# Opening of a one-core decoder layer: weights laid out by channel tile, conditioning rows earlier in the load queue, dummy products first, two evictions behind roundings

## The chip, the core and the metric

The kernel runs on one core of a Trainium2 chip. The core has a matrix engine (PE, with its weight loads shown as PEld), a vector engine (DVE), a scalar engine (ACT), a general engine (POOL) and a queue that issues most transfers (SP). Sixteen DMA engines move data between the chip's memory (HBM) and the core's buffers. PE writes into eight accumulation banks (PSUM), which DVE and ACT read.

The metric is the device time of one execution in microseconds (us), taken as the median of several runs.

## The reference

One layer of a conditioned decoder at batch 1, 256 positions, width 2048, in 32-bit floats:

```
mod = silu(c) @ w_ada + b_ada                 # six vectors of 2048: shift1, scale1, gate1, shift2, ...
h   = rmsnorm(x, g1) * (1 + scale1) + shift1
proj = h @ w_in                               # 2048 -> 10752: lru_x, lru_gate, q, k, v, gate_a, gate_b
y_a = (rg_lru(conv4(lru_x)) * gelu(lru_gate)) @ w_lru_out
y_b = window_attention(q, k, v) @ w_attn_out
x  += gate1 * ((sigmoid(g_a) * y_a + sigmoid(g_b) * y_b) @ w_out)
h2  = rmsnorm(x, g2) * (1 + scale2) + shift2
x  += gate2 * (relu(h2 @ w_ff1) ** 2 @ w_ff2)
out = rmsnorm(x, final_g)
```

What matters here is the first part: the conditioning vectors `mod`, the normed input `h`, and the first products of `w_in`.

## The kernel before, in words

**Tiles.** Channels lie on the 128 partitions, so a width of 2048 is 16 channel tiles (k = 0 to 15) and the 10752 outputs of `w_in` are 84 output tiles (f). An activation tile is 128 x 256. Most products are made with rounded operands: a weight tile is split into a rounded part `wh` (ACT, line 174) and a remainder `wl` (DVE, line 179), an activation into `h[:, 0]` and `h[:, 1]`, and three products replace one (lines 200 to 202). A few products take the plain 32-bit weights as they come from memory; each is then two PE instructions, and needs no rounding.

**Order.** Instructions of the opening are pinned: each engine takes them as they are written in the program. SP issues loads in program order, and a load waits until the buffer that it fills is free. Loads of 1 MB (`raw` tiles: conditioning rows `ra` and weights `rw`) share four buffers.

**The opening** computes all that the first products need:

- SP loads the identity, conditioning row 0 (`ra`, 1 MB), the input x in four pieces of 512 KB (`wh` and `wl` buffers), and row 1. ACT issues two small loads of vectors.
- PE lays silu(c) out along the partitions (16 transposes, line 247), and then runs dummy products of a tile of ones (`WARM`, line 281) that nobody reads.
- DVE multiplies each conditioning row with silu(c) and sums it (`ada_unit`, line 267). Two rows give shift and scale of one channel tile k; `norm1_gain` (line 323) makes the factor.
- x is scaled (lines 295, 297), transposed on PE in four quarters (`turn_in`, line 307) and taken out of PSUM by ACT (`take_in`, line 313).
- For channel tile k, ACT applies factor and shift and rounds (`norm1_tile`, lines 328 and 330); DVE makes the remainder (`norm1_rest`, line 334).
- The "front": ten output tiles (units 0 and 1 of five each) are multiplied with plain weights, one channel tile after the other, as soon as that tile is normed: `front_gemm(0)`, `(1)`, `(2)` (line 361), ten products each into five PSUM banks `fps`. Four of these banks belong to the pool `pg`, which the later products use too.
- `first_part` (line 444) takes the front's sums out of PSUM on ACT, and `split_unit` (lines 174, 179) rounds the weights of unit 2, from which on the products are the rounded ones (`gemm`, lines 200 to 202).

**Passes.** `PASSES` says how the first 56 output tiles are cut: a first pass over channel tiles 0 to 2 (units of five output tiles, a unit being one `raw` load of 128 x 1920), a second pass over channel tiles 3 to 7 (units of three). Between units DVE works off further conditioning rows (`ADA_STEPS`). The remaining channel tiles follow with the rest of the layer, which is not touched.

**Front weights before.** They lie in HBM in the form of units: a partition's row holds, for each output tile, three blocks of 128 floats, one for each channel tile. `front_dma` (lines 351 and 354) picks the blocks of one channel tile out of such rows, in pieces of 512 bytes (the load of 128 x 256 in pieces of 1 KB). It is called for channel tile 0, then, after two conditioning rows, for tiles 1 and 2 together.

Of the kernel before, what the change touches and what calls it, by code (L numbers as in the profile page):

```python
# [10 lines left out]
F32 = mybir.dt.float32  # L11
# [6 lines left out]
P = 128  # L18
T = 256
KT = 16  # L20
# [11 lines left out]
SSD = 4  # L32
WARM = 24

# [7 lines left out]

PASSES = [(0, 3, 56), (3, 8, 56)]
FRONT = 2
PLAIN = {18, 24}
# [17 lines left out]
def hybrid_layer(ctx: ExitStack, tc: tile.TileContext, x, xt, wada, w_p, w_r, w_f, vec, lruw, relb,  # L63
                 onehot, maskc, ident, out):
    nc = tc.nc
# [13 lines left out]
    def nm(s):  # L79
        cnt[0] += 1  # L80
        return f"{s}{cnt[0]}"

    def pair(dt=F32):
        return kp.tile([P, 2, T], dt, tag="k2", name=nm("k"))
# [18 lines left out]
    def ada_dma(pin=same):  # L103
        raw = wp.tile([P, KT * P], F32, tag="raw", name=nm("ra"), bufs=RAW_BUFS)
        pin(nc.sync.dma_start(out=raw, in_=wada[ada_next[0] + len(ada_raw)]))
        ada_raw.append(raw)
# [153 lines left out]
    def ada_unit(pin=same):  # L260
# [8 lines left out]
        return n  # L269

    for q in range(4):
        pc = line_quarter(q)
        o = scr[:, q * 512:(q + 1) * 512]
        if q < 2:
            pin(ve.tensor_copy(o, pc))
        else:
            pin(se.activation(o, pc, AF.Copy))

    wps = pg.tile([P, 2, P], F32, tag="pg", name=nm("pg"))
    for _ in range(WARM):  # L280
        pin(te.matmul(wps[:, 0], lhsT=ones, rhs=ones, start=True, stop=True))
    ada_unit(pin)
# [31 lines left out]

    def warm(n):
        for _ in range(n):
            pin(te.matmul(wps[:, 0], lhsT=ones, rhs=ones, start=True, stop=True))

    h = [None] * KT
# [12 lines left out]
    def norm1_rest(j):  # L332
# [4 lines left out]
    p_units = [(k0, k1, u, min(KT // (k1 - k0), n - u))  # L337
               for k0, k1, n in PASSES for u in range(0, n, KT // (k1 - k0))]
    K1 = PASSES[0][1]
    NF = KT // K1  # L340
    front = {}

    def front_dma(ks):

        t = {k: [pair().rearrange("p a (b m) -> p (a b) m", m=P) for _ in range(FRONT)] for k in ks}
        r = pair().rearrange("p a (b m) -> p (a b) m", m=P)
        n = len(ks)
        src = w_p[0:FRONT, :, 0:NF * K1 * P].rearrange("u p (f k m) -> p u f k m", k=K1, m=P)
        for u in range(FRONT):
            for k in ks:  # L350
                pin(nc.sync.dma_start(out=t[k][u], in_=src[:, u, 0:4, k]))
                for f in range(4):
                    front[u * NF + f, k] = t[k][u][:, f]
            pin(nc.sync.dma_start(out=r[:, u * n:(u + 1) * n], in_=src[:, u, 4, ks[0]:ks[0] + n]))
            for i, k in enumerate(ks):
                front[u * NF + 4, k] = r[:, u * n + i]

# [5 lines left out]

    front_dma([0])
    ada_dma(pin)
    ada_dma(pin)
    front_dma([1, 2])
    scale_in(0, 0)
    scale_in(1, 0)
    turn_in(0)  # L370
    take_in()
    warm(4)
    ada_unit(pin)
# [6 lines left out]
    turn_in(1)  # L380
    ada_dma(pin)
    ada_unit(pin)
    norm1_rest(0)
    ada_unit(pin)
    ada_dma(pin)
    norm1_gain(1)
# [73 lines left out]
    def ask(room):  # L460
        while asked[0] < min(taken[0] + room, len(jobs)):
            i = jobs[asked[0]]
            asked[0] += 1
            if i is None:
                ada_dma(pin)
            else:
                k0, k1, u, nf = p_units[i]
                n = nf * (k1 - k0) * P
                raws[i] = w_dma(w_p[i, :, 0:n], n, pin)

# [52 lines left out]
    split_w = {FRONT: split_unit(FRONT)}  # L523
    take_in()
    for f in range(0, FRONT * NF, 2):
        first_part(fps[f // 2], f)
    open_ps = [None]
    for i in range(FRONT, len(p_units)):
        k0, k1, u, nf = p_units[i]
        if i + 1 < len(p_units):  # L530
            split_w[i + 1] = split_unit(i + 1)
        w = split_w.pop(i)
        for j in range(nf):
# [620 lines left out]
```

## Time and profile before

| what | value |
|---|---|
| median of 3 runs | 1582.1 us (1581.04 to 1583.88) |
| the profiled execution, its own time | 1580.79 us |
| its span (first to last instruction) | 1579.0 us |
| PE busy | 1551.8 us, 98% |
| DVE busy | 1200.7 us, 76% |
| ACT busy | 880.0 us, 56% |
| read from HBM | 384.13 MB, 245 GB/s over the span |

All times below count from the span's first instruction. The profiled execution is 1.8 us longer than its span, and 1.3 us shorter than the median. PE is busy from about the 45th microsecond almost to the end; the share of the first 40th of the span (39.5 us) is 7 tenths, that of all others but the last 9 or more. A row of the timeline or of the chain of waits begins with the start in us and the duration in us. A plain 32-bit product stands there as two PE records, so ten products are 20 records.

### The profile page before, as it was taken

Reading aid. Unit: us, or ns where it says so; the run is one execution under the profiler, and the core shown is the slowest. Engines: PE = TensorE matmul, PEld = TensorE weight load, DVE = VectorE, ACT = ScalarE, POOL = GpSimd, SP = SyncE. Lnnn points to the kernel's source line nnn. Section 1 sums busy time; section 2 is a strip of 40 time slices with the busy share of each in tenths; the row PEclk is TensorE's granted clock in tenths of the full one; section 3 lists DMA queues with packets and bytes.
Section 4 is the critical chain, followed back from the end, with each engine's and each line's share of the span. In section 5 each row is a group of like instructions: output and inputs, shape, how many; then the busy total and the mean of one; then the engine's idle time right before and its main releaser. Section 6 shows DMA issues by size and latency. Waiting matters only on the chain.

```text
span 1579.0 us, 24900 instructions
## 1 busy us (share of the span) xinstructions
PE 1551.8 (98%) x9904; PEld 1393.6 (88%) x9904; DVE 1200.7 (76%) x1841; ACT 880.0 (56%) x1466; POOL 0.2 (0%) x4
## 2 busy tenths in 40 slices
PE   7999999999999999999999999999999999999998
PEld 6999988899988888888889988888888888888887
DVE  5798888899999788798898877865565556655665
ACT  4653457777886564444466763356434663356554
POOL 0000000000000000000000000000000000000000
PEclk9999999999999999999999999999999999999999
DMA  9899976467677768777877666955555555555551
GB/s 362 320 377 344 348 259 222 166 226 254 260 260 277 286 244 298 293 271 290 322 288 260 238 241 242 346 213 188 189 189 190 188 187 190 190 189 188 187 189 57
DMA packets 63717, 387.89 MB, mean 246 GB/s; under 512 B 6800, under 2 KB 14960, under 8 KB 21616
## 3 DMA queue, kind: packets, MB, share of 16 engines
q1 hardware_dynamic: 58896, 381.65, 66.0%
q10 hardware_dynamic: 4704, 4.65, 1.0%
q8 instruction: 77, 1.26, 0.3%
q14 instruction: 40, 0.33, 0.1%
HBM read 384.13 MB, written 2.15 MB: 245 GB/s over the span
## 4 chain that ended last, share of the span: by engine, by line
PE 92%; DVE 4%; DMA 2%; SPq 1%; ACT 1%; issue 0%; DVEq 0%; ACTq 0%
PE pg L214 45%; PE pg L213 22%; PE pg L200 6%; PE pg L202 6%; PE pg L201 5%; PE pg L216 1%; DVE wl L179 1%; PE pg L884 1%; PE pg L885 1%; PE pg L886 1%; DVE ra L267 1%; DVE t L655 1%; PE pg L541 1%; DVE t L682 1%; DMA k<-in_w_p_dram 1%
## 5 line engine op out<-in xcount | busy, mean ns | idle before, releaser
L214 PE MATMUL pg<-k,wh 128*128 128x512 f32 x3088 | 1068.0, 395 | 0.3 <-DVE k L163 0.3
L179 DVE TENSOR_TENSOR wl<-rw,wh 128x1024 fp32r<-128x1024 f32 (+2 forms) x517 | 623.3, 1213 | 276.3 <-ACT wh L174 270.3
L213 PE MATMUL pg<-k,wl 128*128 128x256 f32 x2895 | 810.4, 280 | 0.0
L174 ACT ACTIVATE wh<-rw 128x1024 fp32r<-128x1024 f32 (+2 forms) x517 | 538.7, 1048 | 476.1 <-PE pg L214 327.3
L214 PEld LDWEIGHTS pg<-k,wh 128*128 128x128 f32 x3088 | 566.8, 188 | 119.2 <-PE pg L214 0.6
L213 PEld LDWEIGHTS pg<-k,wl 128*128 128x128 f32 x2895 | 545.1, 188 | 9.7 <-ACT k L162 0.7
L200 PE MATMUL pg<-k,wh 128*128 128x256 f32 x836 | 237.6, 285 | 2.4 <-ACT k L444 1.2
L202 PE MATMUL pg<-k,wl 128*128 128x256 f32 x836 | 235.1, 283 | 2.0 <-DVE wl L179 2.0
L267 DVE CUSTOM_DVE_ANT_0 ra<-ra,scr,vc 128x2048 f32<-128x2048 f32 x96 | 225.2, 2345 | 15.6 <-DMA ra<-in_wada_dram 13.8
L201 PE MATMUL pg<-k,wh 128*128 128x256 f32 x836 | 236.3, 283 | 0.0
L200 PEld LDWEIGHTS pg<-k,wh 128*128 128x128 f32 x836 | 158.3, 189 | 3.9 <-ACT wh L174 1.5
L202 PEld LDWEIGHTS pg<-k,wl 128*128 128x128 f32 x836 | 157.8, 189 | 4.0 <-DVE wl L179 2.2
L201 PEld LDWEIGHTS pg<-k,wh 128*128 128x128 f32 x836 | 158.3, 189 | 0.5 <-issue 0.3
L999 DVE SCALAR_TENSOR_TENSOR k<-pg,mod,k 128x256 f32<-128x256 f32 x124 | 59.9, 483 | 27.8 <-PE pg L214 25.8
L901 ACT ACTIVATE t<-t 128x256 f32<-128x256 f32 x55 | 23.0, 418 | 71.9 <-DVE t L221 71.8
L221 DVE TENSOR_TENSOR t<-pg,t 128x256 f32<-128x256 f32 x131 | 54.7, 417 | 0.3 <-ACT t L220 0.3
L216 PE MATMUL pg<-k,wl 128*128 128x256 f32 x193 | 54.1, 280 | 0.0
L220 ACT ACTIVATE t<-pg 128x256 f32<-128x256 f32 x131 | 47.8, 365 | 0.3 <-PE pg L214 0.3
L216 PEld LDWEIGHTS pg<-k,wl 128*128 128x128 f32 x193 | 36.2, 188 | 8.4
L885 PE MATMUL pg<-z,wh 128*128 128x256 f32 x144 | 40.9, 285 | 0.0
L884 PE MATMUL pg<-z,wh 128*128 128x258 f32 x144 | 40.8, 284 | 0.0
L886 PE MATMUL pg<-z,wl 128*128 128x258 f32 x144 | 40.6, 283 | 0.0
(185 smaller groups left out, 970.5 us busy)
## 6 DMA issues: line engine op xcount, KB each, us to landing
rw<-in_w_f_dram SPq DMA_DIRECT2D x204, 1024.0 KB, 4.8
ra<-in_wada_dram SPq DMA_DIRECT2D x96, 1024.0 KB, 6.3
rw<-in_w_r_dram SPq DMA_DIRECT2D x28, 1024.0 KB, 5.1
rw<-in_w_p_dram SPq DMA_DIRECT2D x27, 960.0 KB, 6.6
bt<-ud ACTq DMA_DIRECT2D x8, 512.0 KB, 4.3
lw<-in_lruw_dram SPq DMA_DIRECT2D x4, 512.0 KB, 5.7
k<-in_x_dram SPq DMA_DIRECT2D x8, 256.0 KB, 5.6
out_dram<-t SPq DMA_DIRECT2D x7, 256.0 KB, 2.6
```

What stands on the lines that cost most here:

```text
L174: pin(se.activation(wh[:, :c], raw[:, o:o + c], AF.Copy))
L179: pin(ve.tensor_tensor(out=wl[:, :c], in0=raw[:, o:o + c], in1=wh[:, :c].bitcast(F32), op=ALU.subtract))
L200: te.matmul(ps, lhsT=wh[:, w], rhs=hl[:, 0], start=k == 0, stop=False)
L201: te.matmul(ps, lhsT=wh[:, w], rhs=hl[:, 1], start=False, stop=False)
L202: te.matmul(ps, lhsT=wl[:, w], rhs=hl[:, 0], start=False, stop=k == n - 1)
L213: te.matmul(ps[:, 0], lhsT=wl[:, w], rhs=hl[:, 0], start=False, stop=False)
L214: te.matmul(ps, lhsT=wh[:, w], rhs=hl, start=k == 0, stop=k == n - 1)
L216: te.matmul(ps[:, 0], lhsT=wl[:, w], rhs=hl[:, 0], start=False, stop=False)
L267: pin(ve.tensor_tensor_reduce(out=raw, in0=raw, in1=scr, scale=1.0, scalar=vc[:, V_BADA + c:V_BADA + c + 1], op0=ALU.mult, op1=ALU.add, ac ...
L884: te.matmul(ps, lhsT=wh[:, e], rhs=z[k][:, 0:258], start=k == 0, stop=False)
L885: te.matmul(ps[:, 0:256], lhsT=wh[:, e], rhs=z[k][:, 258:514], start=False, stop=False)
L999: ve.scalar_tensor_tensor(out=x1[f], in0=ps[:, i], scalar=mod[:, 5 * KT + f:5 * KT + f + 1], in1=x1[f], op0=ALU.mult, op1=ALU.add)
```

## The change

Five edits, all in the opening:

1. **Layout.** The plain weights of the front lie in HBM by channel tile: three rows of `w_p` are added in front, one for each of channel tiles 0, 1, 2, holding ten blocks of 128 floats side by side. `front_dma` loads a channel tile in three pieces (4, 4 and 2 output tiles) of 2 KB, 2 KB and 1 KB for each partition.
2. **Queue order.** The rows for channel tile 2 (`ra_257` and `ra_262` before, `ra_207` and `ra_263` now) stand ahead of the front's weights of tile 2 in SP's queue.
3. **Dummy products.** Six are run ahead of the 16 transposes of silu(c); `WARM` goes from 24 to 26, and the later group of four becomes six.
4. **Evictions.** `take_in` for the last quarter of x moves from ahead of the front's evictions to behind the rounding of unit 3.
5. `PASSES`, `p_units` and the index of `w_p` are adapted to the added rows; later units are loaded as before.

```diff
-WARM = 24
+EARLY, WARM = 6, 26
...
-PASSES = [(0, 3, 56), (3, 8, 56)]
-FRONT = 2
+FRONT, K1 = 2, 3
+NF = KT // K1
+PASSES = [(k, k + 1, FRONT * NF) for k in range(K1)] + [(0, K1, 56), (K1, 8, 56)]
...
+    wps = pg.tile([P, 2, P], F32, tag="pg", name=nm("pg"))
+
+    def warm(n):
+        for _ in range(n):
+            pin(te.matmul(wps[:, 0], lhsT=ones, rhs=ones, start=True, stop=True))
+
+    warm(EARLY)
     for q in range(4):
         pc = line_quarter(q)
...
-    wps = pg.tile([P, 2, P], F32, tag="pg", name=nm("pg"))
-    for _ in range(WARM):
-        pin(te.matmul(wps[:, 0], lhsT=ones, rhs=ones, start=True, stop=True))
+    warm(WARM)
...
-    def front_dma(ks):
-
-        t = {k: [pair().rearrange("p a (b m) -> p (a b) m", m=P) for _ in range(FRONT)] for k in ks}
-        r = pair().rearrange("p a (b m) -> p (a b) m", m=P)
-        n = len(ks)
-        src = w_p[0:FRONT, :, 0:NF * K1 * P].rearrange("u p (f k m) -> p u f k m", k=K1, m=P)
-        for u in range(FRONT):
-            for k in ks:
-                pin(nc.sync.dma_start(out=t[k][u], in_=src[:, u, 0:4, k]))
-                for f in range(4):
-                    front[u * NF + f, k] = t[k][u][:, f]
-            pin(nc.sync.dma_start(out=r[:, u * n:(u + 1) * n], in_=src[:, u, 4, ks[0]:ks[0] + n]))
-            for i, k in enumerate(ks):
-                front[u * NF + 4, k] = r[:, u * n + i]
+    def front_dma(k):
+        n = FRONT * NF
+        t = [pair().rearrange("p a (b m) -> p (a b) m", m=P) for _ in range(0, n, 4)]
+        for f in range(0, n, 4):
+            m = min(4, n - f)
+            pin(nc.sync.dma_start(out=t[f // 4][:, 0:m], in_=w_p[k, :, f * P:(f + m) * P].rearrange("p (f m) -> p f m", m=P)))
+            for i in range(m):
+                front[f + i, k] = t[f // 4][:, i]
...
-    front_dma([0])
+    front_dma(0)
     ada_dma(pin)
     ada_dma(pin)
-    front_dma([1, 2])
+    front_dma(1)
+    ada_dma(pin)
     scale_in(0, 0)
     scale_in(1, 0)
     turn_in(0)
     take_in()
-    warm(4)
+    warm(6)
...
     turn_in(1)
     ada_dma(pin)
+    front_dma(2)
     ada_unit(pin)
     norm1_rest(0)
     ada_unit(pin)
-    ada_dma(pin)
...
     turn_in(3)
     split_w = {FRONT: split_unit(FRONT)}
-    take_in()
     for f in range(0, FRONT * NF, 2):
         first_part(fps[f // 2], f)
...
         if i + 1 < len(p_units):
             split_w[i + 1] = split_unit(i + 1)
+        take_in()
         w = split_w.pop(i)
```

**What it moves in SP's queue.** SP before, from conditioning row 2 to the weights of unit 3 (`ra` are conditioning rows, `k` the front's weights, `rw` the weights of units 2 and 3):

```order
L105 DMA ra_190<-in_wada_dram 128x2048
L105 DMA ra_192<-in_wada_dram 128x2048
L351 DMA k_194<-in_w_p_dram 128x4x128
L351 DMA k_196<-in_w_p_dram 128x4x128
L354 DMA k_198<-in_w_p_dram 128x256
L351 DMA k_195<-in_w_p_dram 128x4x128
L351 DMA k_197<-in_w_p_dram 128x4x128
L354 DMA k_198<-in_w_p_dram 128x256
L105 DMA ra_257<-in_wada_dram 128x2048
L105 DMA ra_262<-in_wada_dram 128x2048
L169 DMA rw_300<-in_w_p_dram 128x1920
L169 DMA rw_302<-in_w_p_dram 128x1920
```

The same place now:

```order
L106 DMA ra_197<-in_wada_dram 128x2048
L106 DMA ra_199<-in_wada_dram 128x2048
L348 DMA k_201<-in_w_p_dram 128x512
L348 DMA k_202<-in_w_p_dram 128x512
L348 DMA k_203<-in_w_p_dram 128x256
L106 DMA ra_207<-in_wada_dram 128x2048
L106 DMA ra_263<-in_wada_dram 128x2048
L348 DMA k_265<-in_w_p_dram 128x512
L348 DMA k_266<-in_w_p_dram 128x512
L348 DMA k_267<-in_w_p_dram 128x256
L170 DMA rw_310<-in_w_p_dram 128x1920
L170 DMA rw_312<-in_w_p_dram 128x1920
```

Rows 4 and 5 (`ra_207`, `ra_263`) went from behind the weights of both tiles to between those of tile 1 and those of tile 2; a channel tile's weights are three loads of whole rows, where six gathered loads held two tiles.

**What it moves on ACT.** ACT before, from the rounding of unit 2 on (L174 rounds weights, L313 takes the transposed x out of PSUM, L444 the front's sums):

```order
L174 ACTIVATE wh_339<-rw_300 128x1024
L174 ACTIVATE wh_341<-rw_300 128x896
L313 ACTIVATE k_348<-pa_325 128x512
L313 ACTIVATE k_350<-pa_330 128x512
L444 ACTIVATE k_352<-pg_230 128x512
L444 ACTIVATE k_354<-pg_231 128x512
L444 ACTIVATE k_356<-pg_232 128x512
L444 ACTIVATE k_358<-pg_233 128x512
L444 ACTIVATE k_360<-pa_234 128x512
L174 ACTIVATE wh_364<-rw_302 128x1024
L174 ACTIVATE wh_366<-rw_302 128x896
```

And now (the same operations are L175, L319 and L439):

```order
L175 ACTIVATE wh_349<-rw_310 128x1024
L175 ACTIVATE wh_351<-rw_310 128x896
L439 ACTIVATE k_358<-pg_236 128x512
L439 ACTIVATE k_360<-pg_237 128x512
L439 ACTIVATE k_362<-pg_238 128x512
L439 ACTIVATE k_364<-pg_239 128x512
L439 ACTIVATE k_366<-pa_240 128x512
L175 ACTIVATE wh_370<-rw_312 128x1024
L175 ACTIVATE wh_372<-rw_312 128x896
L319 ACTIVATE k_378<-pa_335 128x512
L319 ACTIVATE k_380<-pa_340 128x512
```

The two evictions of the last quarter of x stood ahead of the front's five and now stand behind unit 3's rounding. DVE's order is the same as before, and PE's differs by the dummy products and by which buffers the front's products read.

More of the change, by code (lines that the diff above doesn't have):

```diff
@@ L313, in take_in @@
             pin(se.activation(xs[-1].rearrange("p a b -> p (a b)"), turned_in.pop(0), AF.Copy))
-    def warm(n):
-        for _ in range(n):
-            pin(te.matmul(wps[:, 0], lhsT=ones, rhs=ones, start=True, stop=True))
     h = [None] * KT
@@ L337, in hybrid_layer @@
     p_units = [(k0, k1, u, min(KT // (k1 - k0), n - u))
-               for k0, k1, n in PASSES for u in range(0, n, KT // (k1 - k0))]
-    K1 = PASSES[0][1]
-    NF = KT // K1
+               for k0, k1, n in PASSES[K1:] for u in range(0, n, KT // (k1 - k0))]
     front = {}
-    def front_dma(ks):
-        t = {k: [pair().rearrange("p a (b m) -> p (a b) m", m=P) for _ in range(FRONT)] for k in ks}
-        r = pair().rearrange("p a (b m) -> p (a b) m", m=P)
-        n = len(ks)
-        src = w_p[0:FRONT, :, 0:NF * K1 * P].rearrange("u p (f k m) -> p u f k m", k=K1, m=P)
-        for u in range(FRONT):
-            for k in ks:
-                pin(nc.sync.dma_start(out=t[k][u], in_=src[:, u, 0:4, k]))
-                for f in range(4):
-                    front[u * NF + f, k] = t[k][u][:, f]
-            pin(nc.sync.dma_start(out=r[:, u * n:(u + 1) * n], in_=src[:, u, 4, ks[0]:ks[0] + n]))
-            for i, k in enumerate(ks):
-                front[u * NF + 4, k] = r[:, u * n + i]
+    def front_dma(k):
[6 more added lines that the diff above has]
+                front[f + i, k] = t[f // 4][:, i]
     def front_gemm(k):
@@ L468, in ask @@
                 n = nf * (k1 - k0) * P
-                raws[i] = w_dma(w_p[i, :, 0:n], n, pin)
+                raws[i] = w_dma(w_p[K1 + i, :, 0:n], n, pin)
     def take():
```

## The prediction

> **What bounds the kernel now.** I first cut the span into stages. A row holds the stretch in us, its length, then busy us (and records) of PE, PEld, DVE, ACT and POOL, the granted PE clock, the DMA engines' share and GB/s.
>
> ```profile
> 0.00:44.00 44.00, 31.31 (x164) 28.15 (x164) 23.97 (x41) 19.69 (x39) 0.20 (x4) 0.92 0.96 351
> 44.00:94.00 50.00, 49.08 (x416) 48.82 (x416) 43.42 (x47) 34.01 (x54) 0.00 (x0) 1.00 0.87 340
> 94.00:200.00 106.00, 103.70 (x816) 100.83 (x815) 95.27 (x114) 42.86 (x56) 0.00 (x0) 1.00 0.93 355
> ```
>
> From 44 us on PE is the bound: it misses 0.9 us in the next 50. In the opening it misses 12.7 of 44 us, while the DMA engines are 96% busy. A microsecond off the opening is thus a microsecond off the end, if the stage behind follows. Next, what PE waited for up to 300 us (total us, times, longest):
>
> ```profile
> PE pg L361 <- ACT k L328: 5.8, 2, 4.4
> ...
> PE pg L200 <- ACT wh L174: 1.1, 2, 0.8
> ```
>
> The front's products (L361) wait for the normed tile, rounded products (L200) twice for a rounding. The chain of waits, in order of time (start, us), says what stands behind them:
>
> ```profile
> 22.85 7.02 DMA ra<-in_wada_dram
> 29.90 2.35 DVE ra L267
> 32.59 2.26 DVE ra L267
> 35.09 0.61 ACT k L328
> 35.75 5.41 PE pg L361 x16
> ...
> 42.49 1.08 ACT k L313 x2
> 43.58 0.50 ACT k L444
> ```
>
> So the chain is: conditioning row 4 lands at 29.87, DVE works off rows 4 and 5, ACT norms tile 2, PE makes the third ten products, ACT takes the last quarter of x out of PSUM, then the front's first sum, and PE starts the rounded products at 44.12 (43.58 + 0.50 and an issue). I call that start S. Everything turns on the row in the load queue. Loads by their issue (last two numbers of a row) and their time to landing:
>
> ```profile
> L105 SPq DMA_DIRECT2D ra<-in_wada_dram x1: 430/430/430, 12.9 to 12.9; - x1
> ...
> DMA to landing us min/median/max: 9.7/9.7/9.7
> ...
> L105 SPq DMA_DIRECT2D ra<-in_wada_dram x2: 360/371/382, 22.9 to 23.3; - x2
> ...
> DMA to landing us min/median/max: 7.0/8.0/9.0
> ...
> L169 SPq DMA_DIRECT2D rw<-in_w_p_dram x2: 384/894/1403, 23.8 to 25.3; - x2
> ...
> DMA to landing us min/median/max: 10.9/11.3/11.8
> ```
>
> Row 3 lands at 12.9 + 9.7 = 22.6, rows 4 and 5 at 29.9 and 32.3, the weights of units 2 and 3 at 34.7 and 37.1. A 1 MB row takes 32.3 - 29.9 = 2.4 to 2.5 us of a full queue. Between 22.6 and 29.9 pass 7.3 us: one row and the front's weights of tiles 1 and 2, which therefore take 4.8 us, 2.4 us a tile (655 KB, 273 GB/s).
>
> **Layout.** A tile's 655 KB now come in pieces of 2 KB and 1 KB. Their price is not in this trace. The upper end is today's 2.4 us; the lower is the rate of pieces of 7.7 and 8 KB, of which this stretch of the queue (28 to 40 us) consists:
>
> ```profile
> DMA packets 718, 5.04 MB, mean 420 GB/s; under 512 B 80, under 2 KB 80, under 8 KB 452
> ```
>
> 0.655 MB at 420 GB/s is 1.56 us. I take 1.8, nearer to the long pieces, because most pieces grow fourfold. That saves 0.6 us a tile (bounds 0 to 0.85).
>
> **Queue order.** Row 4 no longer has tile 2's weights ahead (2.4 us), and tiles 0 and 1 cost 0.6 less each: it lands 3.6 us earlier, at 26.3; row 5 at 28.75; tile 2's weights at 30.55; units 2 and 3, behind all three tiles, 1.8 earlier, at 32.9 and 35.3. Behind row 5 in SP's queue stand tile 2's weights and both units. Its issue waits until DVE has released row 1's buffer. That is no loss: the queue then still holds rows 2 and 3 and tile 1, up to 6.7 us of transfers, and even today units 2 and 3 are issued 11 us ahead of their landing.
>
> Does the chain follow? DVE is free:
>
> ```profile
> 25.16 0.88 DVE L295 TENSOR_SCALAR wh<-wh,st 128x512 f32<-128x512 f32 x2
> 29.90 2.35 DVE L267 CUSTOM_DVE_ANT_0 ra<-ra,scr,vc 128x2048 f32<-128x2048 f32 x1 [3.86 <-DMA ra<-in_wada_dram]
> ```
>
> It ends its scalings at 26.0 (row 3 comes 0.6 earlier too, so by about 25.5) and idles 3.86 us. Now row 4 runs from 26.3 to 28.65, tile 1's remainder 0.34, and row 5 (there since 28.75) from 29.0. All steps keep their lengths, so the third products start at 35.75 - 3.6 = **32.15**. Late next would be tile 2's weights: 30.55, 1.6 us of room. **3.6 us gained.**
>
> **Clock.** The second and third products are the same work:
>
> ```profile
> 25.93 3.72 PE L361 MATMUL pg<-k,k 128*128 128x256 f32 x16 [1.47 <-ACT k L328]
> ```
>
> 3.72 us against 5.41, because of the clock (last but two of a row):
>
> ```profile
> 15.60:19.00 3.40, 3.35 (x16) 3.28 (x17) 2.78 (x4) 2.12 (x5) 0.00 (x0) 0.50 1.11 391
> 36.20:39.50 3.30, 3.30 (x10) 2.59 (x9) 1.41 (x2) 2.70 (x4) 0.00 (x0) 0.50 1.00 416
> ```
>
> Ahead of the third products PE idled 4.4 us and got half the clock; after 1.47 us of idleness it kept the full one. The second products end 0.6 earlier, with their transposes at about 30.8, so the idle time becomes some 1.4 us, no longer than the case that stayed fast. **1.7 us gained** (bounds 0 and 1.7).
>
> **Evictions.** ACT's timeline around S:
>
> ```profile
> 36.05 1.06 ACT L313 ACTIVATE k<-pa 128x512 f32<-128x512 f32 x2
> 37.00 1.89 ACT L174 ACTIVATE wh<-rw 128x1024 fp32r<-128x1024 f32 x2
> 42.49 1.08 ACT L313 ACTIVATE k<-pa 128x512 f32<-128x512 f32 x2 [3.60 <-PE pa L307]
> ```
>
> ACT idles 3.6 us because the last quarter's transposes stand behind the third products on PE. With that eviction moved, the front's sums follow the rounding. Rounding starts at 33.5 (36.05 + 1.06 less 3.6; unit 2 landed at 32.9), ends at 35.4, and the first sum, long complete, is out at 35.95. DVE's remainders of unit 2 end with it:
>
> ```profile
> 38.09 2.23 DVE L179 TENSOR_TENSOR wl<-rw,wh 128x1024 fp32r<-128x1024 f32 x2 [3.03 <-ACT wh L174]
> ```
>
> 40.3 less 3.5 is 36.8. PE ends the third products and eight transposes (four took 0.45 us) at 32.15 + 3.72 + 0.86 + 0.9 = 37.6, later than both, so it goes on without a wait: **1.2 us gained**. The moved evictions cost ACT 1.06 us behind unit 3's rounding; what they bring out is read only from tile 12 on, and the next sum behind them has over 6 us until its bank is needed.
>
> **Dummy products.** Six ahead are 12 records; at the cold pace of the row at 15.60 (16 in 3.35) 2.5 us, from the moment the ones are written:
>
> ```profile
> 0.83 0.17 DVE L118 MEMSET ones<- 128x128 f32 x1 [0.83 <-PEq L1143]
> ```
>
> They end at about 3.6, where the transposes started at 3.43: 0.2 us late, hidden by DVE's wait for x further on, 1.44 us:
>
> ```profile
> 11.57 0.69 DVE L251 CUSTOM_DVE_ANT_0 t<-wh 128x512 f32<-128x512 f32 x1 [1.44 <-DMA wh<-in_xt_dram]
> ```
>
> They can bring the full clock a few us earlier; nothing that waits for PE there is on the chain. Bounds for the end: 0. The 26 later ones:
>
> ```profile
> 6.90 6.44 PE L281 MATMUL pg<-ones 128*128 128x128 f32 x48
> 15.65 0.45 PE L307 MATMUL pa<-idt,wh 128*128 128x128 f32 x1 [2.32 <-issue]
> ```
>
> If the clock rises sooner they end near 12, earlier than today's 13.3, and PE idles 3.5 instead of 2.32 us before x. The clock then falls there, as it did after 2.32; the four extra records behind (0.9 us cold) delay the first products by up to 0.5. Cover: the 1.47 us of idleness ahead of the second products. Cost 0.
>
> The Trainium skill speaks against this edit (TensorE: Matmul & The Clock Gate, section "Why this matters for your kernels"): no idle gaps over about 3 us, or the clock halves. By it the clock would have survived the 2.32 us and would now be lost; the trace had lost it already, so the sum would be the same by both.
>
> **Sum.** S moves from 44.12 to 37.6: 3.6 + 1.7 + 1.2 = 6.5 us. Behind S, the wait of 1.1 us for a rounding (L174, near 94 us) hangs on buffers that DVE frees, and DVE's stream starts about a microsecond earlier against PE than before. I take 0.4 of it (bounds 0 and 1.1). 6.9 us off the profiled execution's 1580.79 is 1573.9; that execution lies 1.3 below the median, and against the median of 1582.1 it is **1575.2**.
>
> **Rivals.**
>
> *The third products stay cold.* Between 1.47 us of idleness (full clock after) and 2.32 (half) nothing is shown. If my 1.4 is 0.5 too short, or the limit lies lower, the 1.7 are lost: 6.9 - 1.7 = 5.2, 1576.9.
>
> *The layout brings nothing.* Row 4 then lands only 2.4 us earlier, at 27.5, row 5 at 29.9; the products start at 33.35, PE having idled 2 us: 2.4 + 1.2 + 0.4, with or without the 1.7, is 4.0 to 5.7, 1576.4 to 1578.1. For it: the moved row alone does this; against it: 273 GB/s beside 420 in the same queue. The Trainium skill has a rule for it (DMA: Bandwidth & Descriptors, section "Specifications"): from 512 bytes a transfer can run at line rate, so pieces of 512 bytes would gain nothing by growing; the trace disagrees.
>
> *The stage behind gives it back.* If units, not PE, set the pace after S, only unit 3's 1.8 us are kept: 1580.3. For it: the engines of the DMA are 87 to 93% busy there. Against it:
>
> ```profile
> 43.00:49.20 6.20, 5.08 (x43) 5.08 (x44) 2.20 (x3) 5.84 (x12) 0.00 (x0) 1.00 0.24 100
> ```
>
> The queue is three quarters idle for 6 us, as its loads wait for buffers; those come free with S.
>
> *Slower: the clock stays half through all the front.* The price is 1.69 us for some 8 records more than cold already, 0.21 a record; 60 records and 24 transposes (0.1 each) cold put S at about 50.3, which gives 1582.1 + 6.2 = 1588. It decides from some 31 cold records on, when they eat up the 6.5. Against it: both cold stretches ended after one stretch of 3.4 us in which PE was busy.
>
> **How the numbers follow.** Forecast 0.62, cold third products 0.12, layout 0.13, given back 0.08, slower 0.05. The low end takes the bounds together (layout 0.85 for two tiles, 0.5 more; wait 0.7 more) and a microsecond for the runs' spread: 1572.5. The high end takes in the first two rivals with the same spread: 1579.3. Beyond lie 0.13 and the tails. Faster by over 0.2% (about 3 us, what a measurement can tell from no change) is under 1578.9: the first three cases, 0.86; same 0.09; slower 0.05.
>
> **What would show it.** Row 4 landing near 26.3 and DVE's idle time before it gone; third products at 32 at full clock; no eviction between PE's last transpose and L201; S near 37.6. Wrong would be: products waiting for tile 2's weights, a cold row at 32 to 36, or new PE waits between 45 and 100 us.

## The result, and the profile after

| | before | after |
|---|---|---|
| median, runs side by side | 1582.99 us (4 runs) | 1571.81 us (4 runs, 1569.96 to 1573.35) |
| ratio, with its 95% interval | | 0.9926 [0.9903, 0.9948] |
| the same kernel again, later | 1582.13 us (17 runs) | 1572.57 us (5 runs), 0.9936 [0.9923, 0.9949] |
| profiled execution, its span | 1580.79 us, 1579.0 us | 1569.96 us, 1568.2 us |

By the medians the kernel became 11.2 us faster, and 9.6 us in the later runs. I had predicted 6.9 us, and the measured time lies just below the low end of my range (1572.5); the later median lies just inside it. Two executions of the experiments below, 1894.56 us (layout alone) and 1688.36 us (after, one buffer fewer), ran at a granted clock of 0.75 and 0.85 and are left out of the medians. First the part that I did predict. The stages of the changed kernel, cut like those of before (stretch, length, busy us of PE, PEld, DVE, ACT and POOL, PE clock, DMA share, GB/s):

```profile
0.00:37.70 37.70, 31.52 (x183) 29.04 (x184) 24.09 (x41) 20.09 (x40) 0.20 (x4) 0.95 0.97 377
37.70:87.70 50.00, 49.88 (x422) 49.55 (x421) 44.53 (x48) 34.31 (x54) 0.00 (x0) 1.00 0.96 366
87.70:193.70 106.00, 103.99 (x823) 101.47 (x824) 95.63 (x114) 41.70 (x54) 0.00 (x0) 1.00 0.92 357
```

The opening misses 6.2 us of PE where it missed 12.7, and the next 50 us miss 0.1 where they missed 0.9. PE's waits up to 300 us (total, times, longest) say which are left:

```profile
PE pa L313 <- issue: 2.9, 1, 2.9
PE pg L355 <- ACT k L330: 2.2, 2, 1.3
PE pg L203 <- DVE wl L180: 2.0, 1, 2.0
```

The wait for the normed tile fell from 5.8 us to 2.2, and the wait for a rounding (1.1 us) is gone; in the second execution of after, shown as *after, once more* below, 0.7 us of it are back. The chain of waits up to S, in order of time (start, us):

```profile
15.90 10.79 DMA ra<-in_wada_dram
...
26.71 2.35 DVE ra L268
...
29.41 2.26 DVE ra L268
...
31.91 0.61 ACT k L330
...
32.56 3.72 PE pg L355 x16
36.28 0.86 PE pa L355 x4
37.14 0.87 PE pa L313 x8
```

Row 4 lands at 26.69, the third products take 3.72 us at full clock, and behind the last transposes there is no eviction on the chain any more. PE's timeline has no wait ahead of the first rounded product (a wait would stand in brackets, as it does in the first row):

```profile
32.56 3.72 PE L355 MATMUL pg<-k,k 128*128 128x256 f32 x16 [1.27 <-ACT k L330]
...
37.77 0.36 PE L201 MATMUL pg<-k,wh 128*128 128x256 f32 x1
```

S is 37.77; predicted was 37.6. So 6.35 us of the 10.8 us between the two profiled executions came as forecast. The rest arose later. I found it by marks that both traces have: the first product behind PE's 2 us wait near 200 us, the first and the last product on `z` (the feed-forward part's input), and the first product of the last two units. The view of one line's instructions gives the first and the last start. Before:

```profile
L884 PE MATMUL pg<-z,wh x144: 277/283/363, 845.0 to 897.8; 128*128 128x258 f32 x144
...
L910 PE MATMUL pg<-k,wl x32: 276/280/287, 1555.6 to 1561.1; 128*128 128x256 f32 x32
```

After:

```profile
L879 PE MATMUL pg<-z,wh x144: 279/283/367, 836.2 to 889.0; 128*128 128x258 f32 x144
...
L905 PE MATMUL pg<-k,wl x32: 276/281/292, 1544.6 to 1550.2; 128*128 128x256 f32 x32
```

| stretch | before, us | after, us | difference |
|---|---|---|---|
| start to S | 44.12 | 37.77 | -6.35 |
| S to the mark near 200 (199.70; 192.10) | 155.58 | 154.33 | -1.25 |
| mark to the first product on `z` | 645.3 | 644.1 | -1.2 |
| first to last product on `z` | 52.8 | 52.8 | 0 |
| last product on `z` to the last two units: **the long stretch** | 657.8 | 655.6 | -2.2 |
| from there to the end | 23.4 | 23.6 | +0.2 |

The third row is a piece of half clock. Stages of 3.6 us behind the mark, of before and then of after:

```profile
199.70:203.30 3.60, 3.60 (x17) 3.60 (x18) 3.35 (x3) 0.32 (x1) 0.00 (x0) 0.53 0.69 216
```

```profile
192.10:195.70 3.60, 3.60 (x30) 3.60 (x31) 3.35 (x3) 0.95 (x2) 0.00 (x0) 1.00 0.43 155
```

17 products against 30. It came and went between executions of one and the same kernel: before had it in both of its profiled executions (mark to `z` 645.6 us in the second), after in its second alone (644.9). Over all the traces it came in 2 of the 5 of before and its variants with dummy products or an unused buffer, and in 6 of the 10 of after and its variants without dummy products, with an unused buffer or with a shifted ring. So it isn't a gain that belongs to the change.

What decides it can be worked out from the clock records of the traces. In each of the 20 traces the granted clock changes only at times that lie whole multiples of 3.41 us apart (in before at 8.80, 15.63, 19.04, 36.11, 39.52 and 199.95 us), and each execution has this grid of times at another place. The stretch of the grid that holds the wait, and the next one, in the second execution of after and then in the first (PE's busy time is the first one, the clock is third from the end):

```profile
191.07:194.49 3.42, 1.40 (x12) 1.20 (x11) 2.95 (x4) 2.66 (x3) 0.00 (x0) 1.00 0.94 359
194.49:197.90 3.41, 3.41 (x19) 3.41 (x18) 2.62 (x3) 0.00 (x0) 0.00 (x0) 0.50 0.62 197
```

```profile
190.28:193.69 3.41, 1.59 (x13) 1.59 (x14) 3.41 (x5) 1.94 (x3) 0.00 (x0) 1.00 0.65 271
193.69:197.11 3.42, 3.42 (x31) 3.42 (x30) 2.90 (x3) 1.06 (x1) 0.00 (x0) 1.00 0.74 287
```

Both waits last 2.0 us, but PE idles 2.02 us of the one stretch and 1.82 of the other, where the wait had begun in the stretch before. It is the same all through: up to 1555 us, 34 stretches at full clock were followed by half the clock, and in 33 of them PE idles 1.88 us or more, in one 1.54 (after with one buffer fewer, 87.51 to 90.92). Of the stretches that were followed by full clock one has 1.96 us (evictions alone, at 11.57); all others have 1.82 or less. So the idle time within one stretch of the grid goes with the loss, with these two exceptions, and a wait of 2 us loses the clock or keeps it by where the grid lies.

The long stretch is the surprise. No edit touches it, and PE waits for nothing there. The window from 900 to 1540 us, of before and then of after:

```profile
900.00:1540.00 640.00, 640.00 (x3647) 558.74 (x3646) 403.36 (x500) 328.20 (x483) 0.00 (x0) 1.00 0.58 207
```

```profile
900.00:1540.00 640.00, 640.00 (x3661) 560.23 (x3661) 403.64 (x496) 326.78 (x476) 0.00 (x0) 1.00 0.57 204
```

PE is busy throughout at clock 1.00 in both, and yet 14 more products fit into the same 640 us of after. The 3747 products of the stretch and their order on PE are the same.

### The profile page after: what moved, and what is told of

It reads as the page before. It is cut to its first block, busy times and chain, and to the rows that moved or that the text cites. A ratio compares the mean times of both kernels' runs of the same rounds, so it can differ in the third digit from the quotient of the medians.

```text
span 1568.2 us, 24935 instructions
## 1 busy us (share of the span) xinstructions
PE 1548.1 (99%) x9924; PEld 1391.8 (89%) x9924; DVE 1200.9 (77%) x1841; ACT 878.5 (56%) x1466; POOL 0.2 (0%) x4
## 4 chain that ended last, share of the span: by engine, by line
PE 91%; DVE 5%; DMA 1%; ACT 1%; issue 1%; SPq 0%; DVEq 0%; ACTq 0%
PE pg L215 45%; PE pg L214 21%; PE pg L203 6%; PE pg L201 5%; PE pg L202 5%; PE pg L217 1%; DVE wl L180 1%; PE pg L879 1%; PE pg L880 1%; PE pg L881 1%; DVE ra L268 1%; DVE t L650 1%; PE pg L536 1%; DMA k<-in_w_p_dram 1%; DMA ra<-in_wada_dram 1%; PE pa L682 1%
## 5 line engine op out<-in xcount | busy, mean ns | idle before, releaser
L175 ACT ACTIVATE wh<-rw 128x1024 fp32r<-128x1024 f32 (+2 forms) x517 | 538.8, 1048 | 464.3 <-PE pg L215 318.0
```

The costliest lines, as they stand in the source:

```text
L175: pin(se.activation(wh[:, :c], raw[:, o:o + c], AF.Copy))
```

## The experiments

Two questions: which part of the change does what, and what makes PE faster in the long stretch. A table of all runs stands at the end of this section.

### One part at a time

**Layout alone**: before, with the front's weights by channel tile in HBM, and the loads in the old order.

```diff
-    front_dma([1, 2])
+    front_dma(1)
+    front_dma(2)
```

> Layout alone. S is the start of the first rounded product (44.12 us before, 37.77 after). Theory A (each edit pays its own term, at the prices that the trace after shows; what lies behind S only shifts): a tile's weights cost about 1.65 us instead of 2.4, three tiles are ahead of conditioning row 4, so it lands 2.2 us earlier, near 27.6, and the third products start near 33.5; the idle time ahead of them is about 2.2 us, so the clock is a toss-up; the eviction wait of 1.2 us stays. S between 40.2 (full clock) and 41.9 (half clock), the time 2.2 to 3.9 us below before. Rival B (the layout is worth nothing, all comes from the order of the queue): row 4 lands near 29.9, S within 0.5 us of 44.1, no change in time. Rival C (the 4 us that the change gained beyond S belong to the new layout of the buffers and loads): S as in A, the time some 6 to 8 us below before.

**Queue order alone**: before, with the old layout.

```diff
-    front_dma([1, 2])
+    front_dma([1])
+    ada_dma(pin)
...
+    front_dma([2])
     ada_unit(pin)
...
-    ada_dma(pin)
```

> Queue order alone, with the gathered weights. Theory A: row 4 lands 2.4 us earlier, near 27.5, third products near 33.4, tile 2's weights near 32.4, in time; idle ahead of them about 2 us. S 40.0 (full clock) or 41.7 (half clock), the time 2.4 to 4.1 us below before. Rival B (the queue was not what row 4 waited for): row 4 near 29.9, S 44.1, no change. Rival D (tile 2's weights become the late load): third products start when they land, at 33 or later, and wait inside the group.

**Evictions alone**: before, with `take_in()` moved from ahead of the front's sums into the loop over units.

> Evictions alone. Theory A: ACT takes the front's sums out as soon as unit 2 is rounded, PE goes from the transposes straight to the rounded products: S near 42.9, 1.2 us earlier, the time 1.2 us below before (within what can be told from no change). Rival: the moved evictions delay unit 3's stage on ACT, a new PE wait stands between 45 and 60 us, and the time is the same or longer.

**Dummy products alone**: before, with `warm(EARLY)` ahead and 26 and 6 later.

> Dummy products alone. Theory A: nothing on the chain waits for them: S 44.1 plus or minus 0.3, no change in time. Rival E (they keep the clock up where it fell, and that is where the unforeseen 4 us came from): fewer cold records in the opening or behind it, S 1.7 us earlier or more, the time 2 to 4 us below before. The other side: they delay the first products by up to 0.5 us, and the time by as much.

S came to 43.16, 42.64, 42.65 and 44.30 us. The first two are later than the 40.2 to 41.9 and 40.0 to 41.7 that I had expected: row 4 landed at 28.9 and 28.2 us and not near 27.6 and 27.5, and layout and queue order alone leave the third products cold. Their rows, of layout alone and of queue order alone, and the window behind each (clock third from the end):

```profile
34.78 5.41 PE L354 MATMUL pg<-k,k 128*128 128x256 f32 x16 [3.86 <-ACT k L329]
...
35.00:38.40 3.40, 3.40 (x9) 2.70 (x9) 1.27 (x2) 2.93 (x5) 0.00 (x0) 0.51 1.00 418
```

```profile
34.27 5.41 PE L361 MATMUL pg<-k,k 128*128 128x256 f32 x16 [2.58 <-ACT k L328]
...
35.60:39.00 3.40, 3.40 (x10) 2.71 (x9) 2.39 (x3) 1.82 (x3) 0.00 (x0) 0.50 1.01 420
```

Of these waits of 3.86 and 2.58 us, 3.15 and 2.06 lie in the one stretch of the grid ahead of the half clock. Only the two edits together brought the wait down to 1.27 us, and in all twelve traces with both edits the third products ran at full clock. So the clock's 1.7 us belong to neither edit alone. And in these two traces what S had gained was gone at the mark near 200 us, 199.63 and 199.56 us against 199.70 of before (200.84 in its second execution). The evictions alone brought it to 197.62, though S came no earlier than with the queue order. Over nine and ten runs layout and queue order alone are nevertheless 2.8 and 5.2 us faster than before (0.9982 and 0.9967), and the evictions alone 3.0 us (0.9981) where I had expected 1.2. The long stretch accounts for 1.1, 1.7 and 1.1 us of that; where the rest lies, one trace of each doesn't show. The dummy products did nothing that can be measured, 0.9994 [0.9985, 1.0004].

**After, once more**, and **after without the dummy products** (`EARLY, WARM = 0, 24`, later four of six):

> The changed kernel once more, as it is, for more executions and a second profile. Theory A: S within 0.5 us of 37.8, no PE wait of over 0.3 us between 45 and 185 us; the median of the new executions 1571 to 1573. The stretch from the idle time near 568 us to the first product of the last two units (976.6 us in its first profile, 979.1 before) tells how far that number wanders from one execution to the next: theory chance, 976 to 980; theory F (the change took one buffer more out of the ring of 48, which shifts where all later tiles lie), 976 to 977 again.

> The changed kernel with the dummy products as before (none ahead of the transposes, then 24 and 4). Theory A: nothing on the chain waits for them, S 37.8 plus or minus 0.4, the time within 1 us of the changed kernel's. Rival E (they pay for part of the gain): S later or more cold stretches, the time 1 to 3 us longer than the changed kernel's.

S 37.98 and 38.00 us, ratios 0.9936 and 0.9939: the dummy products are worth nothing in the full change either. Without them the third products start behind 2.01 us of idleness and still run at full clock. That was luck in this execution, since the grid (a step at 31.46 us) cut the wait into 0.68 and 1.33 us:

```profile
32.79 3.72 PE L355 MATMUL pg<-k,k 128*128 128x256 f32 x16 [2.01 <-ACT k L330]
```

**After without the evictions edit**:

```diff
     split_w = {FRONT: split_unit(FRONT)}
+    take_in()
     for f in range(0, FRONT * NF, 2):
...
-        take_in()
         w = split_w.pop(i)
```

> After, with the evictions ahead of the first remainders again, as in before. By the prediction's step the edit is worth 1.2 us: S near 39.0, and from S on only a shift, about 1.2 us over after in the median (1573.5 to 1574). Theory (the load loop behind S sets the pace there, and the edit's earlier remainders free the buffers earlier): S near 38.5 to 39.0, the remainders of unit 3 on VectorE start some 2.9 us behind S and not 1 us, a stall of PE of over 1 us comes back between 75 and 95 us, the mark near 200 us (first product behind the wait of 2 us) lies 2 to 3.5 us behind after's 192.1 to 192.2, and the median is 2.5 to 4 us over after's, 1575 to 1577.

1578.63 us, ratio 0.9974 [0.9963, 0.9986]: without this one edit more than half of the gain is lost, 6 us, also more than my theory behind S had expected. S is 39.46, 1.7 us later (0.2 of that are in the start of the third products already); the way from S to the mark near 200 us takes 156.9 us, against 154.3, 155.8 and 154.6 in the three executions above; the long stretch takes 659.0 us instead of 655.6. So 3.4 of the 6 us lie in a stretch that the edit touches only by the choice of buffers (`take_in` takes its buffers later in the program). What sets the stage behind S shows in this kernel's chain of waits, in order of time:

```profile
58.92 2.26 DVE ra L268
61.22 7.98 DMA rw<-in_w_p_dram
69.22 1.90 ACT wh L175 x2
...
83.20 6.24 DMA rw<-in_w_p_dram
89.46 1.91 ACT wh L175 x2
91.42 0.39 PE pg L201
```

DVE frees a buffer, the load into it takes 6 to 8 us, ACT rounds, and only then can PE go on: at these places PE waits for the loop of buffers. From S to the mark such waits for roundings and remainders come to 2.0 us here (the longest 1.7), and to 0 and 1.0 in the two executions of after. The edit lets this loop start earlier. DVE's remainders of unit 3, of before, of after without the edit, and of after:

```profile
47.00 2.23 DVE L179 TENSOR_TENSOR wl<-rw,wh 128x1024 fp32r<-128x1024 f32 x2 [6.34 <-ACT wh L174]
```

```profile
42.34 2.22 DVE L180 TENSOR_TENSOR wl<-rw,wh 128x1024 fp32r<-128x1024 f32 x2 [4.66 <-ACT wh L175]
```

```profile
39.13 2.23 DVE L180 TENSOR_TENSOR wl<-rw,wh 128x1024 fp32r<-128x1024 f32 x2 [1.66 <-ACT wh L175]
```

They start 2.88 us behind S in the first two and 1.36 us behind S in after, as ACT rounds unit 3 before it evicts the last quarter of x.

### What changes the long stretch

The changed front takes its weights into nine buffers (three for each of three channel tiles), where before it took eight. They come from a ring of 48 that later holds all activations, so every later tile lies in another buffer. Adding or removing one buffer that nobody needs tests that.

**Before, with one unused buffer** taken in the front, and **after, with one buffer fewer** (tiles 1 and 2 share the buffer of their last two pieces):

```diff
+    ve.memset(pair()[:, 0, 0:1], 0.0)
```

> The kernel before with one unused buffer more taken out of the ring of 48 at the front's first load (a one-column write on DVE marks it). Theory chance: S 44.1, the stretch behind 576 us 977 to 980, the time that of before. Theory F (placement): the same S, but the stretch some 977, and the time 1.5 to 2.5 us below before.

> The changed kernel with one buffer fewer (the two-tile pieces of channel tiles 1 and 2 share one), so that the ring stands as before. Theory chance: S 37.8, the stretch 976 to 980, the time that of the changed kernel. Theory F: the same S, the stretch some 979, and the time 1.5 to 2.5 us above the changed kernel's.

The long stretch is 654.8 us (before with one more; 657.8 without) and 659.4 us (after with one fewer; 655.6 with it). The window from 900 to 1540 us, of the one and the other, again at full clock and without a wait:

```profile
900.00:1540.00 640.00, 640.00 (x3668) 560.66 (x3667) 406.31 (x505) 330.23 (x488) 0.00 (x0) 1.00 0.58 208
```

```profile
900.00:1540.00 640.00, 640.00 (x3638) 558.38 (x3637) 400.96 (x494) 326.18 (x477) 0.00 (x0) 1.00 0.57 205
```

In the medians only the second shows, 0.9957 against 0.9936, and it can't be put down to the long stretch alone: S is 1.0 us later in its trace, and the way to the mark takes 158.7 us, with 3.4 us of half clock from 90.92 on. In the first the front was late (S 45.38; before's own front comes at 44.12 to 45.17), and its ratio is 0.9992 [0.9983, 1.0001].

These two also touch the front. So the unused buffer was then taken only **ahead of the `z` tiles**, at about 800 us, in after and in before, and before was profiled once more:

> After, with one buffer of the ring of 48 taken and left unused just ahead of the z tiles (at about 800 us), so that every buffer taken from there on is another one; the front and all instructions of TensorE stay as they are. The stretch looked at runs from the first product on z to the first product of the last two units; it was 708.4 us in all three profiled executions that have after's order of buffers (836.2 to 1544.6, 838.7 to 1547.1, 836.7 to 1545.1). Theory (TensorE's pace there depends on which buffers the operands lie in): S within 0.3 us of 37.8, the first product on z at 836 to 839 us, and the stretch anywhere in the 707.5 to 712.5 us that the kernels so far showed, but not at 708.4: off by at least 0.4 us. Rival (the pace comes from something earlier, a phase of the clock or of the queues, that the front leaves behind): 708.4 within 0.2 us.

> Before, with the same unused buffer ahead of the z tiles, so that the stretch has the same count of buffers behind it as in after, but the front is before's. Before's stretch was 710.6 us (845.0 to 1555.6). Theory (which buffers): the stretch is off 710.6 by at least 0.4 us, and if the count of buffers taken ahead is all that counts, it is after's 708.4 within 0.3 us, the median then some 2 us under before's, 1580. Rival (something that the front leaves behind): 710.6 within 0.2 us and a median within 0.7 us of before's.

> Before once more, for what repeats in it. S within 0.3 us of 44.12 (or some 1.2 us later, where the conditioning rows land late), the stretch from the first product on z to the last two units at 710.6 us within 0.2 us if it belongs to the program, and 1 us or more off if it is chance. The stretch of half clock behind the wait of 2 us near 200 us comes or doesn't: both are expected, 1.0 to 1.7 us apart in the time to 576 us.

After with it:

```profile
L880 PE MATMUL pg<-z,wh x144: 277/282/468, 837.7 to 890.8; 128*128 128x258 f32 x144
...
L906 PE MATMUL pg<-k,wl x32: 277/280/285, 1547.6 to 1553.2; 128*128 128x256 f32 x32
```

1547.6 - 890.8 = 656.8 us, 1.2 more than after. Before with it: 656.3, 1.5 less than before, and not after's 655.6, so it isn't the count of buffers alone. Before once more: 657.8, the same to a tenth. The theory held for the stretch. The median of after points the same way (1574.41 us, 0.9950 [0.9933, 0.9966]), but its interval overlaps that of after as it is; that of before shows nothing (1582.21 us, 1.0006 [0.9992, 1.0021]), whose runs here spread over 11 us.

Which property of a buffer counts? Four runs moved the whole ring, and the pools of temporary tiles behind it, and left the choice of buffers alone (`gap`, 32 to 512 bytes, from a pool ahead of the ring), and two moved it far, by another order of the pools:

```diff
+    pad = ctx.enter_context(tc.tile_pool(name="pad", bufs=1))
     kp = ctx.enter_context(tc.tile_pool(name="kp", bufs=48))
...
+    gap = pad.tile([P, 8], F32, name="gap")
```

> After, with 32 bytes per partition left free ahead of the ring of 48 buffers: every tile keeps its buffer and every instruction its place, but all 48 buffers lie 32 bytes further on, so that those that began on a multiple of 64 bytes (every second one, the step being 2080) now don't, and the other way round. The stretch is taken from the last product on z to the first of the last two units: 655.6 us in the three profiled executions of after's order of buffers (889.0 to 1544.6). Theory A (a product's pace depends on whether its moving operand begins on a multiple of 64 bytes): the stretch changes, by 0.5 us or more, here, and is 655.6 again with 64, 128 and 512 bytes. Theory B (it depends on a wider address, a bank or row of the memory): it changes here or not, but changes for 64, 128 or 512. Theory C (it depends on which buffers follow one another, their distance): 655.6 within 0.2 us here and with every pad, since no distance between two buffers changes.

> As the run with 32 bytes, with 64. Theory A (multiple of 64): 655.6 within 0.2 us. Theory B (a wider address): another value, by 0.5 us or more. Theory C (distance between buffers): 655.6 within 0.2 us.

> As the run with 32 bytes, with 128. Theory A: 655.6 within 0.2 us. Theory B: another value where the address matters up to 256 bytes or more. Theory C: 655.6 within 0.2 us.

> As the run with 32 bytes, with 512. Theory A: 655.6 within 0.2 us. Theory B: another value where the address matters at 1 KB or more, 655.6 where its period is 512 or less. Theory C: 655.6 within 0.2 us. In all four S stays within 0.3 us of 37.8, or moves by the chance of when the conditioning rows land.

> After, with the ring of 48 buffers ahead of the weights in memory instead of behind them: the ring lies 65536 bytes per partition lower, the weights 99840 higher, and every tile keeps its buffer of the ring. The stretch from the last product on z to the first of the last two units was 655.6 us in after, 655.0 to 655.6 with the ring 32 to 512 bytes on, and 654.8 to 659.4 over the choices of buffers. Theory (the order in which the ring's buffers are read, their distances, counts): 654.9 to 655.7. Rival (a wide part of the address, or how the moving operand lies to the weights): off by 1 us or more. The median goes with it: after's 1572 within 1 us by the theory, up to 4 us over by the rival.

> After, with the ring behind the temporary tiles: the ring lies 18432 bytes per partition higher, the weights stay, every tile keeps its buffer. Theory: 654.9 to 655.7 us in that stretch and a median within 1 us of after's. Rival: off by 1 us or more; where only the run before shows that, it is the place of the weights that counts and not the ring's.

655.2 and 655.0 us with 32 and 64 bytes, and 655.6 with 128 bytes, 512 bytes, 18 KB and 64 KB. The rows of the last, the ring 64 KB lower:

```profile
L879 PE MATMUL pg<-z,wh x144: 279/283/364, 837.6 to 890.4; 128*128 128x258 f32 x144
...
L905 PE MATMUL pg<-k,wl x32: 276/281/292, 1546.0 to 1551.5; 128*128 128x256 f32 x32
```

So moving the ring by 18 or 64 KB, with or without the weights, changes nothing; 32 and 64 bytes change 0.4 and 0.6 us, which neither theory A nor C had foreseen (B had, for 64); and the choice of buffers within the ring counts for up to 4.6 us. The stretch ahead of `z` answered to the small shifts more strongly. It begins with a product behind a wait of 0.3 us; in after and with 64 bytes:

```profile
568.03 0.47 PE L215 MATMUL pg<-k,wh 128*128 128x512 f32 x1 [0.30 <-DVE k L164]
```

```profile
572.65 0.47 PE L219 MATMUL pg<-k,wh 128*128 128x512 f32 x1 [0.25 <-DVE k L168]
...
L883 PE MATMUL pg<-z,wh x144: 278/283/365, 842.9 to 895.8; 128*128 128x258 f32 x144
```

From there to the first product on `z` after takes 836.2 - 568.03 = 268.2 us and the shift by 64 bytes 842.9 - 572.65 = 270.3; it is 268.7, 268.9 and 268.4 with 32, 128 and 512 bytes, and 268.2 with both far moves, which are multiples of 2 KB. PE waits less than 0.2 us on this way in each of these traces and has the full clock. So the low part of the addresses does count, against theory C in its pure form. Since the ring's step is 2080 bytes, 32 more than 2 KB, another buffer is another low part too; whether all of the 4.6 us is that, these runs don't tell.

| run | S | S to the mark near 200 | long stretch | median of its runs, ratio [95%] |
|---|---|---|---|---|
| before | 44.12 | 155.6 | 657.8 | 1582.99 |
| before once more | 44.55 | 156.3 | 657.8 | (one run, 1582.29) |
| after | 37.77 | 154.3 | 655.6 | 1571.81, 0.9926 [0.9903, 0.9948] |
| after, once more | 37.98 | 155.8 | 655.6 | 1572.57, 0.9936 [0.9923, 0.9949] |
| layout alone | 43.16 | 156.5 | 656.7 | 1578.89, 0.9982 [0.9972, 0.9992] |
| queue order alone | 42.64 | 156.9 | 656.1 | 1577.44, 0.9967 [0.9955, 0.9978] |
| evictions alone | 42.65 | 155.0 | 656.7 | 1578.32, 0.9981 [0.9971, 0.9991] |
| dummies alone | 44.30 | 156.2 | 657.8 | 1581.51, 0.9994 [0.9985, 1.0004] |
| after without dummies | 38.00 | 154.6 | 655.6 | 1573.01, 0.9939 [0.9927, 0.9951] |
| after without evictions | 39.46 | 156.9 | 659.0 | 1578.63, 0.9974 [0.9963, 0.9986] |
| before, unused buffer in front | 45.38 | 156.6 | 654.8 | 1581.24, 0.9992 [0.9983, 1.0001] |
| after, one buffer fewer | 38.79 | 158.7 | 659.4 | 1575.31, 0.9957 [0.9945, 0.9970] |
| after, unused buffer ahead of `z` | 38.4 | 155.5 | 656.8 | 1574.41, 0.9950 [0.9933, 0.9966] |
| before, unused buffer ahead of `z` | 45.17 | 154.8 | 656.3 | 1582.21, 1.0006 [0.9992, 1.0021] |
| after, ring 32 / 64 bytes on | 38.3 / 38.0 | 155.1 / 154.8 | 655.2 / 655.0 | (one run each: 1573.20, 1576.35) |
| after, ring 128 / 512 bytes on | 37.9 / 37.8 | 155.0 / 155.0 | 655.6 / 655.6 | (one run each: 1572.94, 1571.52) |
| after, ring 64 KB lower | 38.4 | 155.0 | 655.6 | 1572.37, 0.9942 [0.9927, 0.9957] |
| after, ring 18 KB higher | 38.3 | 154.5 | 655.6 | 1573.03, 0.9944 [0.9928, 0.9961] |

None is faster than after by more than the intervals.

## Why the prediction was wrong, by its steps

- **Layout**: right. I took 1.8 us a tile. The last front piece lands 1.7 us behind row 5 (issue and time to landing: 17.7 + 11.5 = 29.2, 22.6 + 8.3 = 30.9), 655 KB at 385 GB/s against 273 in pieces of 512 bytes:

```profile
L106 SPq DMA_DIRECT2D ra<-in_wada_dram x1: 328/328/328, 17.7 to 17.7; - x1
...
DMA to landing us min/median/max: 11.5/11.5/11.5
...
L348 SPq DMA_DIRECT2D k<-in_w_p_dram x1: 328/328/328, 22.6 to 22.6; - x1
...
DMA to landing us min/median/max: 8.3/8.3/8.3
```

- **Queue order**: right but 0.4 us too large. Row 4 lands at 26.7 for 26.3, as row 3 landed at 22.6 like before and not the 0.6 us earlier that I had taken for tile 0's weights; the third products start at 32.56 for 32.15. They never wait for tile 2's weights.
- **Clock**: right, 3.72 us at full clock behind 1.27 us of idleness; the runs of one part show that it hangs on layout and queue order together. The rival that the third products stay cold did not come true in after, and did in both single edits. I had compared lengths of waits, and that isn't what decides: it is the idle time in one stretch of the grid of 3.41 us, 1.27 us here, 3.15 and 2.06 in the single edits. Ahead of the transposes of x, waits of 2.99 and 3.13 us (before with an unused buffer, late and in front) kept the full clock, as the grid cut them in two, and 2.32 us in before lost it. A wait of 1.27 us is shorter than the idle time of every stretch that lost the clock. The Trainium skill advises against PE gaps of over about 3 us (TensorE: Matmul & The Clock Gate, section "Why this matters for your kernels"). These traces lost the clock behind 1.96 us (before, near 200 us) and kept it behind 3.13.
- **Evictions**: in S right. ACT's timeline has the order that I had worked out; the first sum is out at 36.20 for 35.95, and the last quarter of x comes out behind unit 3's rounding, after PE's start at 37.77:

```profile
33.81 1.89 ACT L175 ACTIVATE wh<-rw 128x1024 fp32r<-128x1024 f32 x2
35.60 2.06 ACT L439 ACTIVATE k<-pg 128x512 f32<-128x512 f32 x4
...
37.99 1.95 ACT L175 ACTIVATE wh<-rw 128x1024 fp32r<-128x1024 f32 x2
39.78 0.64 ACT L319 ACTIVATE k<-pa 128x512 f32<-128x512 f32 x1
```

- **Dummy products**: right, nothing.
- **Behind S**: this is the step that failed. I took 0.4 us with bounds of 0 and 1.1, from one wait of before, and let everything else only shift, so that the long stretch stood at nothing. The pair of profiled executions gives 4.45 us there, in three pieces. *The long stretch*, 2.2 us: PE's pace follows the choice of buffers, which I had not asked for at all, as I counted only instructions and waits. It repeats in every execution and is, behind S, the largest piece that belongs to the change. It is shown that an unused buffer changes it and that moving the ring by multiples of 2 KB doesn't; it is not shown why. *The stage up to 200 us*, 1.25 us in the pair, and 0.8 between the means (155.7 of four executions, 154.8 to 156.3, of before, twice, with dummy products and with the late unused buffer; 155.0 of ten, 154.3 to 155.8, with after's front): the mechanism that I named (DVE's stream starts earlier, buffers come free earlier) agrees with these runs, and 0.8 lies within my bounds. Without the evictions edit the mark comes at 196.35, with it at 192.1 to 193.9. The rival "the stage behind gives it back" is what the single traces of layout and queue order alone show at the mark; their medians, 2.8 and 5.2 us below before's, say that not all was given back. *Half clock behind the mark*, 1.2 us: luck, as it goes by where the grid lies and came with after's front as well; it is 0.8 us between after's two executions.
- **Sums**: by the terms that it names the low end is 1575.2 less 0.5, 0.7 and 1, 1573.0 and not 1572.5, which the measured time misses all the same, and the high end 1579.1 and not 1579.3. The slower rival's 60 records at 0.21 us and 24 transposes at 0.1 are 15.0 us, which puts S at 52.6 and not 50.3. Nothing else hangs on them.
- The other rivals, a layout that brings nothing and a clock that stays half all through the front, did not come true.

Open is what in the addresses slows PE. Whether a choice exists that is clearly better than after's (654.8 us was the best, found by chance) was not tried further. Nor can the gain be shared out among the four parts, since each of layout, queue order and evictions also changes the choice of buffers.

## What to carry to other kernels

An edit that adds or drops a buffer of a shared ring changes where every later tile lies, and can so change the time of stages that it doesn't touch: compare such stages by marks in both traces before giving their difference to the edit. And a gain at the start of a stage can be lost behind it where the loop that feeds the stage doesn't start earlier too, so ask for the buffer's release and the next load, not only for the engine that is the bound.

## What the runs showed of the hardware that was not expected

- PE, busy all the time at a granted clock of 1.00 and with the same instructions, took from 654.8 to 659.4 us for the same long stretch, 0.7%, depending on which buffers of a ring the tiles lie in; the same kernel repeats to 0.1 us. Moving the whole ring by 18 or 64 KB changes nothing there; 64 bytes took 0.6 us off this stretch and added 2.1 us to the 268 us ahead of it.
- The granted clock changes only on a grid of 3.41 us that lies elsewhere in each execution. Half clock followed where PE idled 1.88 us or more of one such stretch (33 of the 34 times), so a wait of 2.0 us near 200 us lost the clock in some executions of a kernel and not in others, and one of 3.13 us, cut in two by the grid, kept it.
